# Two Strassen layers of an encoder block: a bank for the last product, weight operands made in steps, and weight sums by accumulating transfers

## The chip, the core and the metric

The kernel runs on one core of one Trainium2 chip. The metric is the device time of one execution in microseconds (us). The median of three runs of the kernel before is 1422.38 us (1410.39 to 1423.44).

## The reference, cut to what matters

One DeepNorm encoder block on 1024 tokens of width 1024: an input projection, a gated DeltaNet group beside neighbourhood attention, an output projection, and a squared-ReLU MLP. The change lies in the MLP and in what stands right ahead of it.

```python
mix = jnp.einsum('bte,ed->btd', jnp.concatenate([o_gdn, o_na], axis=-1), w_out[l])
x = layer_norm(DEEPNORM_ALPHA * x + mix, ln1_g[l], ln1_b[l])
ff = jnp.square(jax.nn.relu(jnp.einsum('btd,df->btf', x, w1[l]) + b1[l]))   # 1024 -> 4096
ff = jnp.einsum('btf,fd->btd', ff, w2[l]) + b2[l]                           # 4096 -> 1024
x = layer_norm(DEEPNORM_ALPHA * x + ff, ln2_g[l], ln2_b[l])
```

## The kernel before, in words

Every fp32 operand of a large product is split into a rounded part (fp32r, copied by ScalarE, ACT) and the rest (a subtraction on VectorE, DVE, in `sub_split`, L71). A product is then three matmuls per 128 rows: high by high, high by low, low by high.

**Both MLP layers use Winograd's form of Strassen's scheme:** a 2x2 block product with seven products in place of eight, and sums of the blocks ahead of and behind them.

**First layer.** The 4096 columns are worked in 16 pairs of 128-column blocks (`up_pair(g)`, L1013). The blocks of x (11, 21, 22 and the sums T1 to T4, each 512 channels by 512 tokens) are made once, in the stretch in which the output projection and the LayerNorm end (L944 to L974). For each pair `w1_raw` loads 1 MiB of w1, `w_ops` forms the four sums S1 to S4 (L898 to L901, DVE) and splits seven weight operands (L882 ACT, L71 DVE). The seven products have 12 matmuls each (L910 to L912): psA (11), psB6, psC7, psE5, again psA (12 times 21), psD4, and the last one, S4 times 22, which adds into psE5's bank. That bank is read by h22 = u3 + pe (L1035) ahead of it, so the last product waits for that read. Sums, bias and squared ReLU follow on DVE and ACT, and seven blocks of 256 KB go to `h_d` in DRAM (L1059). The first two products of pairs 0 and 1 are made early, between the transposes of x.

**Weight sums of the second layer.** `w2_sums(g)`, called in every pair, loads blocks of w2 (L1002, 2 x 256 KB per half pair), forms four sums on GpSimd (POOL, L1003 to L1006) and stores them in `t_d` in DRAM (L1007, 512 KB), two halves per pair, each with one buffer.

**Second layer.** Seven products in four groups of four pairs are 28 steps. Step n loads 1 MiB of `h_d` and 1 MiB of w2 or of `t_d` (`down_ops`, L1080), splits both (L1083 ACT, L71 DVE), and makes 48 matmuls (L1181 to L1183). Loads are issued two steps ahead; raw buffers turn over every three steps and the five operand tiles (`x`) hold two and a half steps.

All DMAs of the kernel before are issued by the SP queue, in order. A scheduler that simulates the program sets each engine's order; each engine then runs its own order strictly.

Of the kernel before, what the change touches and what calls it, by code (L numbers as in the profile page):

```python
# [15 lines left out]
P = 128  # L16
# [20 lines left out]
def tile_trunk(ctx: ExitStack, tc: tile.TileContext, A: dict, out: bass.AP):  # L37
# [817 lines left out]
    t_d = dr.tile([4, NG, P, 512], F32, name="t_d")  # L855
# [9 lines left out]
    for nm in ("T4", "22"):  # L865
        X[nm] = bigp.tile([P, 2, 4, 512], F32R, tag="big", name="x" + nm, bufs=2)
# [7 lines left out]
    def utile(name):  # L874
        return wk.tile([P, 512], F32, tag="u", name=name, bufs=4)
# [18 lines left out]
    def w_ops(raw, have=()):  # L894

        q11, q12, q21, q22 = (w_quad(raw, a, k) for a in range(2) for k in range(2))
        s1, s2, s3, s4 = (tmp(f"ws{i}").rearrange("p (k c) -> p k c", k=4) for i in range(4))
        V.tensor_tensor(s1, q21, q22, ALU.add)  # L898
        V.tensor_tensor(s2, s1, q11, ALU.subtract)
        V.tensor_tensor(s3, q11, q21, ALU.subtract)  # L900
        V.tensor_tensor(s4, q12, s2, ALU.subtract)  # L901
        w = dict(have)
        for nm, src in (("11", q11), ("S2", s2), ("S3", s3), ("S1", s1), ("12", q12), ("22", q22), ("S4", s4)):
            if nm not in w:
                w[nm] = w_split(src)
        return w
# [34 lines left out]
    raw1 = [tmp("w1q").rearrange("p (k c) -> p k c", k=4) for k in range(2)]  # L941
    for k in range(2):
        D.dma_start(raw1[k], A["w1"][k * 512:k * 512 + 512, 2 * P:3 * P].rearrange("(kt p) c -> p kt c", p=P))
    for hf in range(2):  # L944
        for q in range(4):
            t = hf * 4 + q
            out_proj(t, oTn[1][:, :, t * P:(t + 1) * P], wo1[0][2:4], wo1[1][2:4], oo, "o", G, nb=4)
            layer_norm(t, wk)
        for kt in range(NK) if hf == 0 else (0, 4, 1, 5, 2, 6, 3, 7):
            ps = psC.tile([P, 512], F32, tag="t", name="psx1", bufs=2)  # L950
            for q in range(4):
                mm = TE.transpose(ps[:, q * P:(q + 1) * P], yacc[hf * 4 + q][:, kt * P:(kt + 1) * P], ident)
            turns.append(mm)
            full = hold8("x1f") if hf == 0 else tmp("x1s")
            S.activation(full, ps, AF.Identity, bias=l1b[:, kt:kt + 1], scale=l1g[:, kt:kt + 1])
            k = kt % 4
            if hf == 0:
                full0[kt] = full
                x_split("11" if kt < 4 else "21", k, full, (S, V)[kt % 2], (V, G)[kt % 2])
                continue  # L960
            full1[kt] = full
            if kt < 4:
                continue
            b11, b12, b21, b22 = full0[k], full1[k], full0[kt], full
            x_split("22", k, b22, S, G)
            t1, t3 = tmp("t1"), tmp("t3")
            V.tensor_tensor(t1, b12, b11, ALU.subtract)
            V.tensor_tensor(t3, b22, b12, ALU.subtract)
            x_split("T1", k, t1, S, V)
            x_split("T3", k, t3, S, V)  # L970
            V.tensor_tensor(b22, b22, t1, ALU.subtract)
            x_split("T2", k, b22, S, V)
            V.tensor_tensor(b21, b21, b22, ALU.subtract)
            x_split("T4", k, b21, S, G)  # L974


    wops = {0: {}, 1: {}}
    for nm, src in (("11", w_quad(raw0, 0, 0)), ("12", w_quad(raw0, 0, 1))):
        wops[0][nm] = w_split(src)
    for nm, src in (("11", raw1[0]), ("12", raw1[1])):  # L980
        wops[1][nm] = w_split(src)
    early = {}
    pace = pacer(turns[NK:], 22, 3)
    for g in range(2):
        ps = bank("s", "psA")
# [4 lines left out]
    for g in range(2):  # L990
        prod(early[g][0], wops[g]["12"], X["21"], False, pace)
    close(oo)
    w2p = open_pool("w2p")
    wops[0] = w_ops(raw0, wops[0])

    def w2_sums(g):
        for hc in range(2):
            c = slice(hc * 256, hc * 256 + 256)
            r = w2p.tile([P, 2, 2, 256], F32, tag="r", name="w2r", bufs=1)
            t = w2p.tile([P, 4, 256], F32, tag="t", name="w2s", bufs=1)  # L1000
            for k in range(2):
                D.dma_start(r[:, k], A["w2"][(2 * g + k) * P:(2 * g + k + 1) * P, :].rearrange("p (j c) -> p j c", j=2)[:, :, c])  # L1002
            G.tensor_tensor(t[:, 0], r[:, 0, 1], r[:, 0, 0], ALU.subtract)  # L1003
            G.tensor_tensor(t[:, 1], r[:, 1, 1], t[:, 0], ALU.subtract)  # L1004
            G.tensor_tensor(t[:, 2], r[:, 1, 1], r[:, 0, 1], ALU.subtract)  # L1005
            G.tensor_tensor(t[:, 3], r[:, 1, 0], t[:, 1], ALU.subtract)  # L1006
            D.dma_start(t_d[:, g, :, c].rearrange("i p c -> p i c"), t)  # L1007
# [5 lines left out]
    def up_pair(g, mid=None):  # L1013
        if g + 1 < NG:
            wops[g + 1] = w_ops(w1_raw(g + 1), wops.get(g + 1, ()))
        w = wops.pop(g)
        f = 2 * g
        if g in early:
            pa, u2 = early[g]
        else:  # L1020
            pa = bank("s", "psA")
            prod(pa, w["11"], X["11"])
            u2 = utile("p1")
            S.activation(u2, pa, AF.Copy)
        pb = bank("p", "psB6")
        prod(pb, w["S2"], X["T2"])
        V.tensor_tensor(u2, u2, pb, ALU.add)
        pc = bank("t", "psC7")
        prod(pc, w["S3"], X["T3"])
        u3 = utile("u3")  # L1030
        V.tensor_tensor(u3, u2, pc, ALU.add)
        pe = bank("p", "psE5")
        prod(pe, w["S1"], X["T1"])
        h22 = hold8("h22")
        V.tensor_tensor(h22, u3, pe, ALU.add)  # L1035
        act2(h22, h22, f + 1)
        if mid is not None:
            mid()
        if g not in early:
            prod(pa, w["12"], X["21"], False)  # L1040
        h11 = hold8("h11")
        act2(h11, pa, f)
        pd = bank("o", "psD4")
        prod(pd, w["22"], X["T4"])
        h21 = hold8("h21")
        V.tensor_tensor(h21, u3, pd, ALU.add)
        act2(h21, h21, f + 1)
# [6 lines left out]
        V.tensor_tensor(s1, h12, h22, ALU.add)  # L1054
        V.tensor_tensor(s2, s1, h11, ALU.subtract)
        V.tensor_tensor(s3, h11, h12, ALU.subtract)
        V.tensor_tensor(s4, h21, s2, ALU.subtract)
        for i, h in enumerate((h11, h21, h22, s1, s2, s3, s4)):
            D.dma_start(h_d[i, g], h)  # L1059
# [4 lines left out]
    right = [t_d[i].rearrange("g p c -> p g c") for i in range(4)]  # L1064
    order = [(left[0], w2q[0, 0]), (left[4], right[1]), (left[5], right[2]), (left[3], right[0]),
             (left[2], right[3]), (left[1], w2q[1, 0]), (left[6], w2q[1, 1])]
# [3 lines left out]
    def down_ops(n):  # L1070
        i, gr = divmod(n, NQ)
        sl = slice(gr * 4, gr * 4 + 4)
        if n % 3 == 0:
            raws = [raw8().rearrange("p a (k c) -> p (a k) c", c=512) for j in range(2)]
        else:
            r = bigp.tile([P, 2, 4, 512], F32, tag="big", name="d2r", bufs=2)
            raws = [r[:, j] for j in range(2)]
        res = []
        for src, raw in zip(order[i], raws):
# [14 lines left out]
    close(w2p)  # L1094
# [202 lines left out]
```

## Time and profile before

| | |
|---|---|
| median of 3 runs | 1422.38 us |
| profiled execution | 1419.53 us, of which the span is 1417.7 us |
| mean granted TensorE clock | 0.964 |
| busy in the span: PE (TensorE) / DVE / ACT / POOL | 1303.8 / 920.5 / 639.1 / 336.5 us |
| first layer's products, first to last | 714.17 to 1098.46 us |
| second layer's products | from 1098.46 us |

Matmuls overlap, so the busy time of PE says only whether it had work; the granted clock beside it says at which of the two levels, 1.2 or 2.4 GHz, it ran. The sum of a stretch is best read from the starts of its first and last matmul.

### The profile page before, as it was taken

Reading aid. Unit: us, or ns where it says so; the run is one execution under the profiler, and the core shown is the slowest. Engines: PE = TensorE matmul, PEld = TensorE weight load, DVE = VectorE, ACT = ScalarE, POOL = GpSimd, SP = SyncE. Lnnn points to the kernel's source line nnn. Section 1 sums busy time; section 2 is a strip of 40 time slices with the busy share of each in tenths; the row PEclk is TensorE's granted clock in tenths of the full one; section 3 lists DMA queues with packets and bytes.
Section 4 is the critical chain, followed back from the end, with each engine's and each line's share of the span. In section 5 each row is a group of like instructions: output and inputs, shape, how many; then the busy total and the mean of one; then the engine's idle time right before and its main releaser. Section 6 shows DMA issues by size and latency. Waiting matters only on the chain.

```text
span 1417.7 us, 20015 instructions
## 1 busy us (share of the span) xinstructions
PE 1303.8 (92%) x7318; PEld 1082.8 (76%) x7318; DVE 920.5 (65%) x1543; ACT 639.1 (45%) x1224; POOL 336.5 (24%) x356
## 2 busy tenths in 40 slices
PE   5999999999999967999966898998799999999996
PEld 4688888878888856898745676776688788888885
DVE  6756897922368457557778766656565695555955
ACT  5457666334332253455464344353455443334431
POOL 3000001011123139223476344443300000000403
PEclk9999999989999997999987899999999999999998
DMA  6233547468776698653344677777746975555731
GB/s 188 57 110 111 141 137 170 119 135 253 229 218 201 174 343 194 172 170 100 104 144 130 231 259 231 255 232 258 233 163 223 393 270 191 207 199 178 246 111 60
DMA packets 240579, 267.27 MB, mean 189 GB/s; under 512 B 38865, under 2 KB 169809, under 8 KB 240481
## 3 DMA queue, kind: packets, MB, share of 16 engines
q1 hardware_dynamic: 240480, 265.99, 60.5%
q8 instruction: 58, 0.95, 0.3%
q14 instruction: 41, 0.33, 0.1%
HBM read 180.94 MB, written 85.00 MB: 188 GB/s over the span
## 4 chain that ended last, share of the span: by engine, by line
PE 39%; DMA 13%; DVE 7%; POOL 6%; issue 3%; ACT 2%; SPq 1%; DVEq 0%; POOLq 0%; ACTq 0%
DMA w2r<-in_w_dram 7%; PE psdn L1182 6%; PE psdn L1183 6%; PE psdn L1181 6%; DMA wraw<-in_w_dram 3%; PE po L754 2%; PE psop L802 2%; PE psop L804 2%; PE psop L803 2%; POOL w2s L1004 1%; POOL w2s L1006 1%; POOL w2s L1005 1%; POOL w2s L1003 1%; PE pt L747 1%; DMA B<-in_rpbT_dram 1%
## 5 line engine op out<-in xcount | busy, mean ns | idle before, releaser
L1182 PE MATMUL psdn<-d,d 128*128 128x512 f32 (+1 forms) x464 | 177.3, 383 | 0.8 <-DVE d L71 0.7
L1183 PE MATMUL psdn<-d,d 128*128 128x512 f32 (+1 forms) x464 | 177.1, 382 | 0.0
L1181 PE MATMUL psdn<-d,d 128*128 128x512 f32 (+1 forms) x464 | 175.1, 382 | 0.4 <-ACT d L1083 0.4
L71 DVE TENSOR_TENSOR d<-d2r,d 128x1024 fp32r<-128x1024 f32 x72 | 85.7, 1238 | 62.9 <-ACT d L1083 62.9
L1083 ACT ACTIVATE d<-d2r 128x1024 fp32r<-128x1024 f32 x72 | 71.4, 1049 | 113.0 <-PE psdn L1183 91.9
L1182 PEld LDWEIGHTS psdn<-d,d 128*128 128x128 f32 x464 | 87.3, 188 | 18.5 <-DVE d L71 1.6
L1181 PEld LDWEIGHTS psdn<-d,d 128*128 128x128 f32 x464 | 87.2, 188 | 17.7 <-ACT d L1083 0.8
L1183 PEld LDWEIGHTS psdn<-d,d 128*128 128x128 f32 x464 | 87.3, 188 | 16.6
L93 POOL TENSOR_TENSOR lrs<-lrs,mhalf 128x1 f32<-128x1 f32 x8 | 6.4, 804 | 347.8 <-DVE lrs L1123 347.8
L1010 ACT ACTIVATE h<-h,b1T 128x512 f32<-128x512 f32 x48 | 34.5, 719 | 104.2 <-DVE h L1035 76.2
L120 PE MATMUL psj<-xlo,whi 128*128 128x512 f32 x192 | 77.0, 401 | 1.8 <-DVE xlo L71 1.8
L119 PE MATMUL psj<-xhi,whi 128*128 128x512 f32 x192 | 76.4, 399 | 0.7 <-DVE xhi L170 0.7
L121 PE MATMUL psj<-xhi,wlo 128*128 128x512 f32 x192 | 75.9, 395 | 0.0
L1003 POOL TENSOR_TENSOR w2s<-w2r 128x256 f32<-128x256 f32 x32 | 29.2, 911 | 154.3 <-DMA w2r<-in_w_dram 154.3
L71 DVE TENSOR_TENSOR d<-wraw,d 128x1024 fp32r<-128x1024 f32 x40 | 47.6, 1234 | 27.8 <-ACT d L1083 27.8
L71 DVE TENSOR_TENSOR wlo<-wraw,whi 128x1024 fp32r<-128x1024 f32 x28 | 34.3, 1223 | 47.4 <-ACT whi L110 42.5
L240 DVE SCALAR_TENSOR_TENSOR cy<-hraw,convw,cy 128x1024 f32<-128x1024 f32 x48 | 61.2, 1280 | 5.6 <-ACT cy L238 4.5
L1083 ACT ACTIVATE d<-wraw 128x1024 fp32r<-128x1024 f32 x40 | 39.9, 1048 | 49.0 <-PE psdn L1183 41.5
L882 ACT ACTIVATE w1t<-ws 128x512 fp32r<-128x512 f32 x64 | 39.7, 625 | 48.3 <-PE psC L912 23.0
L898 DVE TENSOR_TENSOR ws<-wraw 128x512 f32<-128x512 f32 x16 | 11.0, 689 | 75.2 <-DMA wraw<-in_w_dram 75.2
L754 PEld LDWEIGHTS po<-vt,et 128*128 128x128 f32 x384 | 52.3, 198 | 8.7 <-ACT et L752 3.5
L754 PE MATMUL po<-vt,et 128*128 128x64 f32 x384 | 51.8, 275 | 5.1 <-ACT et L752 2.6
(341 smaller groups left out, 3679.3 us busy)
## 6 DMA issues: line engine op xcount, KB each, us to landing
wraw<-in_w_dram SPq DMA_DIRECT2D x21, 1024.0 KB, 7.0
d2r<-h_d SPq DMA_DIRECT2D x18, 1024.0 KB, 5.4
w2r<-in_w_dram SPq DMA_DIRECT2D x64, 256.0 KB, 4.3
t_d<-w2s SPq DMA_DIRECT2D x32, 512.0 KB, 3.9
h_d<-hs SPq DMA_DIRECT2D x64, 256.0 KB, 2.5
wraw<-in_w_in_dram SPq DMA_DIRECT2D x28, 512.0 KB, 4.7
h_d<-h SPq DMA_DIRECT2D x48, 256.0 KB, 5.4
d2r<-t_d SPq DMA_DIRECT2D x11, 1024.0 KB, 7.7
```

Source lines behind the costliest of these rows:

```text
L71: return eng.tensor_tensor(lo, full, f32(hi), ALU.subtract)
L119: pace(TE.matmul(ps, hi[:, kt], xhi[:, kt, sl], start=(kt == 0), stop=False))
L120: pace(TE.matmul(ps, hi[:, kt], xlo[:, kt, sl], start=False, stop=False))
L121: pace(TE.matmul(ps, lo[:, kt], xhi[:, kt, sl], start=False, stop=(kt == NK - 1)))
L240: V.scalar_tensor_tensor(y, raw[:, i:i + T], convw[:, ci, i:i + 1], y, ALU.mult, ALU.add)
L754: mm = TE.matmul(po[:, j], et[:, c], vts[j][:, t + c, e * 64:e * 64 + 64], start=(c == 0), stop=(c == 2))
L882: S.activation(t[:, 0], src, AF.Copy)
L1003: G.tensor_tensor(t[:, 0], r[:, 0, 1], r[:, 0, 0], ALU.subtract)
L1083: S.activation(t[:, 0, k], raw[:, k], AF.Copy)
L1181: TE.matmul(ps, h[:, 0, k, qs_], w[:, 0, k, c], start=(start and k == 0), stop=False)
L1182: TE.matmul(ps, h[:, 0, k, qs_], w[:, 1, k, c], start=False, stop=False)
L1183: TE.matmul(ps, h[:, 1, k, qs_], w[:, 0, k, c], start=False, stop=(stop and k == 3))
```

## The change

- **Last product:** P3 (S4 times 22) has a bank of its own (`psF3`). u2 takes psE5 by one more addition on DVE, and h12 is u2 + psF3. psA's bank alternates between two tags; the four other products share two tags.
- **First products early for four pairs** in place of two (`NE = 4`, 256 KB loads `w1q` of the pairs 1 to 3).
- **Weight operands one by one:** `w_steps` yields after each operand, and a step is written behind each join of the pair before; the 1 MiB of w1 is loaded one pair earlier.
- **x blocks:** the second token half is kept in `xs`; T1 and 22 are made first. In pair 0 the products go in the order 5, 3, 7, 6, 4. All low parts there, and those of the last output projection, are made on DVE and none on POOL.
- **Second layer's weights:** `w2_sums`, its loads, POOL sums, stores and `t_d` are gone. `down_ops` loads one block of w2 and adds 0, 2, 1, 1, 3, 0, 0 more (products 0 to 6, four steps each: 28 in all) by transfers that POOL issues and that add to the raw tile. Some sums of h and the final additions change sign for it.

```diff
-    t_d = dr.tile([4, NG, P, 512], F32, name="t_d")
...
-    def w_ops(raw, have=()):
+    def w_steps(raw, w):
...
+        V.tensor_tensor(s1, q21, q22, ALU.add)
+        put("11", q11)
+        yield
+        V.tensor_tensor(s2, s1, q11, ALU.subtract)
+        put("S2", s2)
+        yield
...
+    NE = 4
...
-            out_proj(t, oTn[1][:, :, t * P:(t + 1) * P], wo1[0][2:4], wo1[1][2:4], oo, "o", G, nb=4)
+            out_proj(t, oTn[1][:, :, t * P:(t + 1) * P], wo1[0][2:4], wo1[1][2:4], oo, "o", V, nb=4)
...
+            if kt < 4:
+                V.tensor_tensor(full0[k], full, full0[k], ALU.subtract)
+                x_split("T1", k, full0[k], S, V)
+            else:
+                x_split("22", k, full, S, V)
...
-    def w2_sums(g):
-        for hc in range(2):
-            c = slice(hc * 256, hc * 256 + 256)
...
-            D.dma_start(t_d[:, g, :, c].rearrange("i p c -> p i c"), t)
...
+        if g + 2 < NG:
+            raws1[g + 2] = w1_raw(g + 2)
+        steps = w_steps(raws1.pop(g + 1), wops[g + 1]) if g + 1 < NG else iter(())
...
-        prod(pe, w["S4"], X["22"], False)
-        h12 = hold8("h12")
-        V.tensor_tensor(h12, u2, pe, ALU.add)
-        act2(h12, h12, f)
-        w2_sums(g)
+        def p3():
+            pf = bank("t", "psF3")
+            prod(pf, w["S4"], X["22"])
+            return pf
...
+        def join5(pe):
+            V.tensor_tensor(h22, u3, pe, ALU.add)
+            V.tensor_tensor(u2, u2, pe, ALU.add)
+            act2(h22, h22, f + 1)
+            step()
...
-    order = [(left[0], w2q[0, 0]), (left[4], right[1]), (left[5], right[2]), (left[3], right[0]),
-             (left[2], right[3]), (left[1], w2q[1, 0]), (left[6], w2q[1, 1])]
+    d11, d12, d21, d22 = (w2q[k, j] for k in range(2) for j in range(2))
+    order = [(left[0], (d11,)), (left[4], (d22, d12, d11)), (left[5], (d22, d12)), (left[3], (d12, d11)),
+             (left[2], (d22, d12, d11, d21)), (left[1], (d21,)), (left[6], (d22,))]
...
-            D.dma_start(raw, src[:, sl])
+            D.dma_start(raw, src[0][:, sl])
+            for more in src[1:]:
+                G.dma_start(raw, more[:, sl], accum_op=ALU.add)
```

The order of DVE before, in the middle of the first layer (ws are the sums of the next pair, out of its load wraw; p, u and h are the joins of this pair with the banks psB, psC and psE, and hs sums of h):

```order
L898 TENSOR_TENSOR ws_9655<-wraw 128x512
L1054 TENSOR_TENSOR hs_9465<-h_9443,h_9395 128x512
L899 TENSOR_TENSOR ws_9656<-ws_9655,wraw 128x512
L71 TENSOR_TENSOR w1t<-ws_9483,w1t 128x512
L1055 TENSOR_TENSOR hs_9466<-hs_9465,h_9411 128x512
L1056 TENSOR_TENSOR hs_9467<-h_9411,h_9443 128x512
L900 TENSOR_TENSOR ws_9657<-wraw 128x512
L1027 TENSOR_TENSOR p_9524<-p_9524,psB_9526 128x512
...
L1031 TENSOR_TENSOR u_9553<-p_9524,psC_9540 128x512
L901 TENSOR_TENSOR ws_9658<-wraw,ws_9656 128x512
L71 TENSOR_TENSOR w1t<-ws_9482,w1t 128x512
L1035 TENSOR_TENSOR h_9568<-u_9553,psE_9555 128x512
```

The same place in the change:

```order
L903 TENSOR_TENSOR ws_9469<-wraw 128x512
L906 TENSOR_TENSOR ws_9470<-ws_9469,wraw 128x512
L1114 TENSOR_TENSOR hs_9280<-h_9166,h_9167 128x512
...
L1049 TENSOR_TENSOR p_9310<-p_9310,psB_9325 128x512
L909 TENSOR_TENSOR ws_9471<-wraw 128x512
L71 TENSOR_TENSOR w1t<-ws_9314,w1t 128x512
L1081 TENSOR_TENSOR u_9320<-p_9310,psC_9343 128x512
L918 TENSOR_TENSOR ws_9472<-wraw,ws_9470 128x512
L71 TENSOR_TENSOR w1t<-ws_9312,w1t 128x512
L1085 TENSOR_TENSOR h_9323<-u_9320,psE_9361 128x512
L1086 TENSOR_TENSOR p_9310<-p_9310,psE_9361 128x512
```

The sums of the next pair still stand ahead of the joins; what moved is the load behind wraw, which is issued a pair earlier, and the addition to p (L1086) that frees psE's bank from the last product.

The order of SP before around such a load (t_d is what POOL has summed, w2r the blocks for the next half):

```order
L1059 DMA h_d<-h_9395 128x512
L1007 DMA t_d<-w2s 128x4x256
L1002 DMA w2r<-in_w_dram 128x2x256 x2
L888 DMA wraw<-in_w_dram 128x8x256
L1059 DMA h_d<-h_9411 128x512
```

In the change only the seven stores to `h_d` and the load stand there, so nothing on SP waits for POOL in the first layer.

The order of POOL in the change in the second layer. It has no other instruction until the final LayerNorms; d2r_10253 is the weight tile of step 4, d2r_10316 of step 5, wraw_10392 of step 6, then steps 7, 8, 9, 10 and 11:

```order
L1143 DMA d2r_10253<-in_w2_dram 128x4x512
L1143 DMA d2r_10316<-in_w2_dram 128x4x512
L1143 DMA wraw_10392<-in_w2_dram 128x4x512
L1143 DMA d2r_10253<-in_w2_dram 128x4x512
L1143 DMA d2r_10316<-in_w2_dram 128x4x512
L1143 DMA wraw_10392<-in_w2_dram 128x4x512
L1143 DMA d2r_10455<-in_w2_dram 128x4x512
L1143 DMA d2r_10518<-in_w2_dram 128x4x512
L1143 DMA d2r_10455<-in_w2_dram 128x4x512
L1143 DMA wraw_10581<-in_w2_dram 128x4x512
L1143 DMA d2r_10655<-in_w2_dram 128x4x512
L1143 DMA d2r_10717<-in_w2_dram 128x4x512
```

Each waits until what is in its tile has landed, so the second addition of step 4 stands behind the first ones of the steps 5 and 6.

## Rows read from the trace of the kernel before

**Rows 1.** The page's 40 slices: busy tenths of PE

```profile
PE   5999999999999967999966898998799999999996
```

**Rows 2.** Busy time by stretch (length, engines, clock, DMA share, GB/s)

```profile
714.17:757.00 42.83, 20.11 (x80) 14.64 (x79) 34.10 (x37) 22.93 (x38) 30.43 (x27) 0.70 0.33 108
803.00:1098.46 295.46, 271.82 (x1136) 219.54 (x1136) 185.86 (x268) 134.23 (x218) 90.13 (x96) 0.95 0.70 230
714.17:1098.46 384.29, 332.96 (x1376) 266.71 (x1374) 251.14 (x349) 176.34 (x288) 142.02 (x140) 0.92 0.66 215
1096.00:1140.00 44.00, 43.52 (x191) 35.31 (x190) 29.98 (x30) 21.21 (x24) 0.00 (x0) 1.00 1.02 383
1160.00:1360.00 200.00, 200.00 (x884) 165.72 (x883) 128.78 (x145) 76.17 (x80) 15.89 (x12) 1.00 0.62 218
```

**Rows 3.** Waits of PE, 690 to 1160 us (total, times, longest)

```profile
PE psE L910 <- DVE h L1035: 22.3, 7, 7.4
PE psB L910 <- ACT w1t L882: 19.1, 1, 19.1
```

**Rows 4.** Chain of waits, 985 to 1020 us (start, us, what)

```profile
994.89 0.75 POOL w2s L1006
995.65 0.38 SPq L1007
...
997.46 9.46 DMA wraw<-in_w_dram
...
1015.97 0.61 DVE h L1035
```

**Rows 5.** Waits of DVE (first row) and SP (second) in the first layer

```profile
DVE ws L898 <- DMA wraw<-in_w_dram: 75.2, 13, 10.8
SPq L1007 <- POOL w2s L1006: 108.5, 31, 12.5
```

**Rows 6.** Timeline of DVE and, last, of POOL

```profile
704.93 0.42 DVE L937 CAST x<-x1f 128x512 fp32r<-128x512 f32 x1
744.25 0.68 DVE L71 TENSOR_TENSOR xT<-t,xT 128x512 fp32r<-128x512 f32 x1
744.86 1.75 DVE L967 TENSOR_TENSOR t<-x1s,x1f 128x512 f32<-128x512 f32 x1
758.71 6.68 POOL L71 TENSOR_TENSOR xT<-x1f,xT 128x512 fp32r<-128x512 f32 x1 [4.05 <-ACT xT L935]
```

**Rows 7.** Timeline of PE: first matmuls of products and of pairs

```profile
838.16 0.40 PE L910 MATMUL psA<-x,w1t 128*128 128x512 f32 x1
...
1016.62 0.79 PE L910 MATMUL psE<-x,w1t 128*128 128x512 f32 x1 [7.39 <-DVE h L1035]
...
1021.52 0.39 PE L910 MATMUL psA<-x,w1t 128*128 128x512 f32 x1
...
1040.74 0.40 PE L910 MATMUL psA<-x,w1t 128*128 128x512 f32 x1
...
1059.98 0.40 PE L910 MATMUL psA<-x,w1t 128*128 128x512 f32 x1
```

**Rows 8.** Timeline of SP: loads of the steps 1, 4 and 6

```profile
1095.85 0.37 SPq L1080 DMA_DIRECT2D d2r<-h_d  x1
...
1114.29 2.23 SPq L1080 DMA_DIRECT2D d2r<-t_d  x1
...
1130.80 2.43 SPq L1080 DMA_DIRECT2D wraw<-t_d  x1
```

**Rows 9.** The page's DMA issues (count, KB each, us to landing)

```profile
d2r<-h_d SPq DMA_DIRECT2D x18, 1024.0 KB, 5.4
d2r<-t_d SPq DMA_DIRECT2D x11, 1024.0 KB, 7.7
```

**Rows 10.** The page's costliest groups: the splits of the second layer

```profile
L71 DVE TENSOR_TENSOR d<-d2r,d 128x1024 fp32r<-128x1024 f32 x72 | 85.7, 1238 | 62.9 <-ACT d L1083 62.9
L1083 ACT ACTIVATE d<-d2r 128x1024 fp32r<-128x1024 f32 x72 | 71.4, 1049 | 113.0 <-PE psdn L1183 91.9
```

More of the change, by code (lines that the diff above doesn't have):

```diff
@@ L864, in tile_trunk @@
         X[nm] = xp.tile([P, 2, 4, 512], F32R, tag="x", name="x" + nm, bufs=5)
-    for nm in ("T4", "22"):
+    xs = bigp.tile([P, 2, 4, 512], F32, tag="big", name="xs", bufs=2)
+    for nm in ("22", "T4"):
         X[nm] = bigp.tile([P, 2, 4, 512], F32R, tag="big", name="x" + nm, bufs=2)
@@ L874, in utile @@
     def utile(name):
[L875 removed]
+        return wk.tile([P, 512], F32, tag="u", name=name, bufs=5)
     def bank(tag, name):
@@ L892, in w_quad, with put @@
         return raw[:, k * 4:k * 4 + 4, a * P:(a + 1) * P]
-    def w_ops(raw, have=()):
+    def w_steps(raw, w):
         q11, q12, q21, q22 = (w_quad(raw, a, k) for a in range(2) for k in range(2))
         s1, s2, s3, s4 = (tmp(f"ws{i}").rearrange("p (k c) -> p k c", k=4) for i in range(4))
[L898 to L903, printed above, removed]
+        def put(nm, src):
             if nm not in w:
                 w[nm] = w_split(src)
-        return w
+        V.tensor_tensor(s1, q21, q22, ALU.add)
[4 more added lines that the diff above has]
+        yield
+        V.tensor_tensor(s3, q11, q21, ALU.subtract)
+        put("S3", s3)
+        yield
+        put("S1", s1)
+        yield
+        put("12", q12)
+        yield
+        put("22", q22)
+        yield
+        V.tensor_tensor(s4, q12, s2, ALU.subtract)
+        put("S4", s4)
+        yield
     def prod(ps, w, x, first=True, pace=lambda mm: None):
@@ L962, in tile_trunk, with bank_a @@
             if kt < 4:
[L963 to L977, printed above, removed]
+                V.tensor_tensor(full0[k], full, full0[k], ALU.subtract)
+                x_split("T1", k, full0[k], S, V)
+            else:
+                x_split("22", k, full, S, V)
+    for k in range(4):
+        t1, b12, b21, b22 = full0[k], full1[k], full0[4 + k], full1[4 + k]
+        V.tensor_tensor(b12, b22, b12, ALU.subtract)
+        x_split("T3", k, b12, S, V)
+        V.tensor_tensor(t1, b22, t1, ALU.subtract)
+        x_split("T2", k, t1, S, V)
+        V.tensor_tensor(b21, b21, t1, ALU.subtract)
+    for k in range(4):
+        x_split("T4", k, full0[4 + k], S, V)
+    def bank_a(g):
+        return bank("sp"[g % 2], "psA")
+    wops = {g: {} for g in range(NG)}
     for nm, src in (("11", w_quad(raw0, 0, 0)), ("12", w_quad(raw0, 0, 1))):
         wops[0][nm] = w_split(src)
-    for nm, src in (("11", raw1[0]), ("12", raw1[1])):
-        wops[1][nm] = w_split(src)
+    for g in range(1, NE):
+        for nm, k in (("11", 0), ("12", 1)):
+            wops[g][nm] = w_split(rawq[g, k])
     early = {}
     pace = pacer(turns[NK:], 22, 3)
-    for g in range(2):
-        ps = bank("s", "psA")
+    for g in range(NE):
+        ps = bank_a(g)
         prod(ps, wops[g]["11"], X["11"], True, pace)
@@ L989, in tile_trunk @@
         early[g] = ps, u
-    for g in range(2):
-        prod(early[g][0], wops[g]["12"], X["21"], False, pace)
+        if g % 2:
+            for e in (g - 1, g):
+                prod(early[e][0], wops[e]["12"], X["21"], False, pace)
     close(oo)
-    w2p = open_pool("w2p")
-    wops[0] = w_ops(raw0, wops[0])
-    def w2_sums(g):
-        for hc in range(2):
-            c = slice(hc * 256, hc * 256 + 256)
[L999 to L1006, printed above, removed]
-            D.dma_start(t_d[:, g, :, c].rearrange("i p c -> p i c"), t)
+    raws1 = {0: raw0}
+    for _ in w_steps(raw0, wops[0]):
+        pass
+    raws1[1] = w1_raw(1)
     def act2(h, src, f):
@@ L1013, in up_pair, with step @@
     def up_pair(g, mid=None):
-        if g + 1 < NG:
-            wops[g + 1] = w_ops(w1_raw(g + 1), wops.get(g + 1, ()))
+        if g + 2 < NG:
+            raws1[g + 2] = w1_raw(g + 2)
+        steps = w_steps(raws1.pop(g + 1), wops[g + 1]) if g + 1 < NG else iter(())
+        def step():
+            next(steps, None)
         w = wops.pop(g)
@@ L1020, in up_pair @@
         else:
-            pa = bank("s", "psA")
+            pa = bank_a(g)
             prod(pa, w["11"], X["11"])
@@ new lines, in up_pair, with p6, p7, p5 @@
+        h11, h21, h22, h12 = (hold8(x) for x in ("h11", "h21", "h22", "h12"))
+        def p6():
+            pb = bank("o", "psB6")
+            prod(pb, w["S2"], X["T2"])
+            V.tensor_tensor(u2, u2, pb, ALU.add)
+            step()
+        def p7():
+            pc = bank("t", "psC7")
+            prod(pc, w["S3"], X["T3"])
+            return pc
+        def p5():
+            pe = bank("o", "psE5")
+            prod(pe, w["S1"], X["T1"])
+            return pe
+        def p2():
+            if g not in early:
+                prod(pa, w["12"], X["21"], False)
+            act2(h11, pa, f)
+            step()
@@ new lines, in p4, with join7 @@
+        def p4():
+            pd = bank("t", "psD4")
+            prod(pd, w["22"], X["T4"])
+            V.tensor_tensor(h21, u3, pd, ALU.add)
+            act2(h21, h21, f + 1)
+            step()
+        def p3():
+            pf = bank("t", "psF3")
+            prod(pf, w["S4"], X["22"])
+            return pf
+        def join7(pc):
+            V.tensor_tensor(u3, u2, pc, ALU.add)
+            step()
+        def join5(pe):
+            V.tensor_tensor(h22, u3, pe, ALU.add)
+            V.tensor_tensor(u2, u2, pe, ALU.add)
+            act2(h22, h22, f + 1)
+            step()
@@ new lines, in join3 @@
+        def join3(pf):
+            V.tensor_tensor(h12, u2, pf, ALU.add)
+            act2(h12, h12, f)
+            step()
+        if g == 0:
+            pe, pf = p5(), p3()
+            pc = p7()
+            p6()
+            join7(pc)
+            join5(pe)
+            p4()
+            p2()
+            join3(pf)
+        else:
+            p6()
+            join7(p7())
+            join5(p5())
+            if mid is not None:
+                mid()
+            p2()
+            p4()
+            join3(p3())
```

60 lines of the change are left out of this document (19 added, 41 removed).

## The prediction

> **What bounds the kernel now.** I read the page's slices first, then the stretches of the MLP, then who waited for whom, and last the chain of waits. The slices show PE full from the 30th on, where the second layer runs, and between 0.6 and 0.9 in the first layer [rows 1]. The stretches put numbers on it [rows 2]. In the second layer 884 matmuls fill 200 us, 0.226 us each at a granted clock of 1.00, that is 2.4 GHz; a step of 48 takes 10.86 us and nothing waits. In the first layer, 384.29 us long, PE is idle for 384.29 - 332.96 = 51.3 us, and the granted clock is 0.92 on average: after waits PE runs for a while at the lower level, 1.2 GHz. A pair without a wait takes 1059.98 - 1040.74 = 19.24 us for 84 matmuls, 0.229 us each [rows 7]. Sixteen such pairs are 307.8 us; the 32 transposes between them (1376 records less 1344) add some 4 (an estimate, half a matmul's time each). So 72 us of the stretch are waits and their low clock.
>
> The waits have two owners [rows 3]: one of 19.1 us at the start, while the x operands are made, and seven of the last product for h22 on DVE, 22.3 us in all. The chain shows what lies behind the second kind [rows 4]: POOL ends a sum, SP stores it, only then SP reaches the load of w1, which takes 9.46 us; DVE, which has the next pair's sums ahead of this pair's joins, stands still for it, and PE waits for the join. DVE lost 75.2 us to that load in 13 waits, SP 108.5 us to POOL in 31 [rows 5].
>
> **The change, part by part.** *Start of the first layer.* Before, the last product of pair 3 ends at 838.16 us [rows 7]. In the change about 153 DVE instructions stand between the first CAST of x, at 704.93 us, and pair 3's last join. Without POOL beside it DVE issues one every 0.61 us; next to a POOL subtraction the same form takes 1.75 in place of 0.68 us, and POOL's own took up to 6.68 [rows 6]. POOL's splits move to DVE, so its cost is in the count: 153 x 0.61 = 93, which ends at 798. PE needs 336 x 0.229 + 4 = 81 us from 714.17, to 795; the four early pairs give it 96 matmuls, 22 us, for the time in which it waited 19.1. The later bound with 5 us for arrivals is 803: a gain of 35.
>
> *Pairs 4 to 15.* Before they take 1098.46 - 838.16 = 260.3 us, without waits 12 x 19.24 = 230.9: a gain of 29. The load of w1 now has a pair's time ahead of its use. DVE's 21 instructions per pair (4 sums, 7 splits, 6 joins, one more than before, 4 sums of h) are 13 to 14 us at 0.61 to 0.68, hidden under 19.24; if a load came late again, they would be what is late. Removing POOL's 128 sums, their loads and stores has no further price: POOL was on PE's path only through SP.
>
> Of these 64 us I count 56: 8 for about four new waits of 2 us with their low clock, and for low parts of the output projection that DVE now makes ahead of 704.93. Bounds: 40, if the start gains only 11, and 68.
>
> *Second layer.* The 28 steps have 28 more transfers of 1 MiB on the same 16 engines, and POOL issues them in a strict order. No row shows an accumulating transfer. The nearest is a plain load: 383 GB/s at a share of 1.02 [rows 2] make 2.75 us per MiB, and 5.4 us to landing [rows 9] leave 2.65 us of latency. The lower end is 2.75, if only what is read from DRAM counts; the upper is 5.5, if the tile that is read back counts as much. I take the lower end, since the plain load of the same block is the nearest row, and keep both for the range.
>
> First, step 4. Its second addition stands behind the first one of step 6 on POOL, and that waits for step 6's load. From step 1's load at 1095.85 to step 6's at 1130.80 [rows 8] SP issues 16.75 MiB: 12 for the steps 1 to 6, 2.5 of constants, 1 of y and 1.25 of h. They take 46.1 us, and step 6 lands at 1095.85 + 46.1 + 2.65 = 1144.6, 46 us into the second layer. Two first additions in between make it 51.6; step 6's first and step 4's second addition, with latency, 59.8; half a split is 1.05 + 1.24 us [rows 10], so 62. PE wants step 4 after 4 x 10.86 = 43.4: a wait of 18 us. Second, product 4 (steps 16 to 19) needs 5 MiB per step, 13.75 us against 10.86, 11.6 us in all; loads run up to three steps ahead and have room in the products 2 and 3 (8.25 us per step), so I count half, 6. Third, two waits cost clock: after the wait of 7.39 us twelve matmuls took 1021.52 - 1016.62 = 4.9 us in place of 2.75 [rows 7], so 4 for two. Together 28 us.
>
> The additions and subtractions that change sign cost nothing: the same instructions in the same places.
>
> **Sum.** The profiled execution took 1419.53 us (span 1417.7), 2.85 under the median. 1419.5 - 56 + 28 = 1391 us.
>
> In the trace, plain transfers fill the engines at 383 GB/s [rows 2], and that alone gave my price. The Trainium skill (Collectives: The Full Stack, The bandwidth ceiling: the fold count and why AG ≠ RS ≠ AR) says of a transfer that adds on its way: "it's slower because the add needs **two source reads**", about half the rate of a copy. No run here shows it; by that rule the price would be the upper end, and the sum the first rival's.
>
> **Rivals.** *1. The additions bind the second layer; slower.* At 5.5 us each, the engines must carry up to step 19 16.75 + 26 plain MiB at 2.75 and 28 additions at 5.5: 117.6 + 154 = 271.6 us from 1095.85, so step 19 is ready 274 us into the layer, against 19 x 10.86 = 206 on PE. That is 68 us late, and some four waits' clock make it 76: 1419.5 - 56 + 76 = 1440. For it: the tile has to be read as well as w2, and the engines were already full for 44 us at the start of this layer. Against: their share is 0.62 later on [rows 2]. Between the ends the loss grows by (76 - 28) / 2.75 = 17.5 us per us of price; it eats the 56 at about 4.35 us, which is the point from which it decides. The page's rule above is this rival's, and its only support.
>
> *2. Gain and loss cancel.* A price near 4.1 costs 28 + 1.35 x 17.5 = 52: 1415 us. Or the first layer gains only 40, because DVE's order waits for x operands at the start: 1407. For it: DVE is the later bound there.
>
> *3. The transfers are hidden anyway.* If the additions fit under the loads, 1419.5 - 56 = 1363. For it: 0.62 of the engines' time is used in the steady part. Against: POOL's order ties step 4 to step 6 whatever the price.
>
> That the change leaves the first layer as it was is unlikely: in its order the last product has its own bank, and no load on SP stands behind POOL.
>
> **How the numbers follow.** The forecast (1375 to 1405) has a chance of 0.40, rival 3 0.10, rival 2 0.22, rival 1 0.28. A measurement of this kernel can tell about 1%, 14 us, from no change. Faster by over 1% (under 1408) are the forecast and rival 3, 0.50; within 1% 0.22; slower 0.28. The range goes from rival 3 with a first-layer gain of 64, 1356, to rival 1 with some 10 us less gain, 1450; it leaves out dearer additions still and a first layer that gains nearly nothing. Both signs hold much of the chance; the forecast's own range is 1375 to 1405.
>
> **What would show it.** In the new profile: waits of the last product for DVE gone, and the first layer's products over some 328 us long; DVE no longer waiting 75 us for w1; a wait of PE of about 18 us at step 4 and short ones at steps 16 to 19, ended by splits that waited for a POOL transfer. Waits of 10 us or more at each of the steps 16 to 19, with the DMA share near 1 there, would show rival 1. The prediction is wrong if the additions' landing time is far from 5.4 us, or if DVE holds PE in the first pairs.

## The result, and the profile after

The change takes 1429.17 us (median of 20 runs, 1424.31 to 1437.71) against 1422.36 us of the kernel before (20 runs): a ratio of 1.0084, 95% interval 1.0061 to 1.0108. The forecast was 1391, faster; the result is slower, clear of noise but by under 1%, and lies between the first rival's 1440 and the second rival's 1415. The profiled execution took 1434.19 us, span 1432.4. The two profiled executions differ by 14.7 us and the medians by 6.8: single executions of one kernel spread over more than 10 us, so the stretches below are those of one profile each.

Two stretches explain it. The first layer runs from the first matmul of its products (psA) to the first of the second layer (psdn), the second layer from there to the end of the span:

| kernel | first psA at | first layer | second layer | span |
|---|---|---|---|---|
| before | 714.2 | 384.3 | 319.2 | 1417.7 |
| the change | 712.8 | 325.6 | 394.0 | 1432.4 |
| difference | -1.4 | -58.7 | +74.8 | +14.7 |

The runs 1, 2 and 6 below have the change's first layer unaltered, and it took 326.3, 325.8 and 325.0 us there: this stretch repeats within some 1 us. The first layer gained what was forecast, the second lost 75 in place of 28. The page's slices of the change (tenths; PE, granted clock, DMA) show where: the waits stood before in the slices 21 to 29 [rows 1]; now that part is full, and holes stand where PE had been full.

```profile
PE   5999999999999966999998999999993899866996
PEclk9999999999999988999998999999996989978998
DMA  6233557469776796663314545444699999999731
```

The stretches of the change (length, busy time of PE, PEld, DVE, ACT, POOL, then clock, DMA share, GB/s), which answer to [rows 2]:

```profile
712.00:803.00 91.00, 81.38 (x349) 63.91 (x350) 79.28 (x133) 56.43 (x95) 4.16 (x6) 0.94 0.35 111
803.00:1038.00 235.00, 235.00 (x1027) 192.46 (x1026) 158.79 (x249) 124.20 (x197) 0.00 (x0) 1.00 0.51 167
1038.00:1330.00 292.00, 228.83 (x954) 185.82 (x953) 140.68 (x142) 83.62 (x88) 36.40 (x28) 0.89 1.04 275
1330.00:1420.00 90.00, 90.00 (x443) 76.37 (x441) 64.47 (x82) 34.37 (x38) 24.59 (x18) 1.00 0.41 149
```

From 803 us on PE has no idle time left in the first layer, at 2.4 GHz. In the second layer the DMA engines are full for 292 us (share 1.04) while they move 275 GB/s; full engines moved 383 before [rows 2]. So the bytes that are counted are not what fills them. When the last addition is done, PE runs full to the end. The matmuls of PE that had waited, in the timeline:

```profile
1106.19 2.07 PE L1243 MATMUL psdn<-d,d 128*128 128x512 f32 x4 [24.08 <-ACT d L1146]
...
1148.23 2.08 PE L1243 MATMUL psdn<-d,d 128*128 128x512 f32 x4 [7.49 <-ACT d L1146]
...
1258.69 2.08 PE L1243 MATMUL psdn<-d,d 128*128 128x512 f32 x4 [9.52 <-ACT d L1146]
...
1279.32 0.80 PE L1243 MATMUL psdn<-d,d 128*128 128x512 f32 x1 [7.31 <-ACT d L1146]
...
1305.80 2.08 PE L1243 MATMUL psdn<-d,d 128*128 128x512 f32 x4 [12.81 <-ACT d L1146]
...
1320.88 1.21 PE L1243 MATMUL psdn<-d,d 128*128 128x512 f32 x4 [1.45 <-ACT d L1146]
```

Counted in steps of 10.86 us from 1038.4, the first stands ahead of step 4 (1038.4 + 43.4 + 24.1 = 1105.9), the second of step 7, the last four of the steps 16 to 19. With 0.5 for a low part they are 63.2 us; the other 11.6 of the 74.8 are matmuls at the lower clock after them. The queues of the change between 1038 and 1330 us (packets, MB, share of the 16 engines' time; q0 is POOL's, q1 SP's), and two of the issues (us to landing):

```profile
q0 software_dynamic: 14784, 29.36, 55.1%
q1 hardware_dynamic: 24794, 50.81, 48.3%
...
d2r<-in_w_dram POOLq DMA_DIRECT2D x20, 1024.0 KB, 13.4
...
d2r<-in_w_dram SPq DMA_DIRECT2D x15, 1024.0 KB, 11.9
```

The 28 additions took 0.551 x 292 = 160.9 us of all engines, 5.75 us each; the 48.5 MiB of plain transfers 141 us, 2.91 each. The price is the upper end of the prediction's bounds, and a little more. The figures are shares of engines that are full; no run shows an addition on idle engines.

### The profile page after: what moved, and what is told of

Read it like the earlier page. It is cut to its first block, busy times and chain, and to the rows that moved or that the text cites. A ratio compares the mean times of both kernels' runs of the same rounds, so it can differ in the third digit from the quotient of the medians.

```text
span 1432.4 us, 19819 instructions
## 1 busy us (share of the span) xinstructions
PE 1299.7 (91%) x7318; PEld 1079.5 (75%) x7318; DVE 913.2 (64%) x1579; ACT 641.2 (45%) x1224; POOL 226.5 (16%) x236
## 3 DMA queue, kind: packets, MB, share of 16 engines
HBM read 194.58 MB, written 68.22 MB: 183 GB/s over the span
## 4 chain that ended last, share of the span: by engine, by line
PE 45%; DMA 15%; DVE 6%; issue 3%; ACT 1%; POOL 1%; SPq 0%; DVEq 0%; ACTq 0%; POOLq 0%
DMA d2r<-in_w_dram 10%; PE psdn L1243 3%; PE psdn L1244 3%; PE psdn L1245 3%; PE psA L926 2%; PE psA L924 2%; PE psA L925 2%; DMA wraw<-in_w_dram 2%; PE po L754 2%; PE psop L802 2%; PE psop L804 2%; PE psop L803 1%; PE psF L924 1%; PE psD L924 1%; PE psD L926 1%
## 5 line engine op out<-in xcount | busy, mean ns | idle before, releaser
L1243 PE MATMUL psdn<-d,d 128*128 128x512 f32 (+1 forms) x464 | 180.5, 399 | 62.7 <-ACT d L1146 62.7
L1244 PE MATMUL psdn<-d,d 128*128 128x512 f32 (+1 forms) x464 | 180.3, 389 | 0.5 <-DVE d L71 0.5
L1245 PE MATMUL psdn<-d,d 128*128 128x512 f32 (+1 forms) x464 | 179.6, 387 | 0.0
L71 DVE TENSOR_TENSOR d<-d2r,d 128x1024 fp32r<-128x1024 f32 x72 | 89.9, 1295 | 107.8 <-ACT d L1146 107.8
L1243 PEld LDWEIGHTS psdn<-d,d 128*128 128x128 f32 x464 | 90.6, 197 | 82.9 <-ACT d L1146 65.2
L1143 POOL DMA_DIRECT2D d2r<-in_w_dram x20 | 26.6, 1359 | 519.0 <-DMA bB<-in_ln_b_dram 347.8
L1244 PEld LDWEIGHTS psdn<-d,d 128*128 128x128 f32 x464 | 89.4, 193 | 19.2 <-DVE d L71 1.5
L1245 PEld LDWEIGHTS psdn<-d,d 128*128 128x128 f32 x464 | 89.1, 192 | 17.6
L743 ACT ACTIVATE ex<-sn,nm 128x384 f32<-128x384 f32 x64 | 39.0, 609 | 33.9 <-DVE nm L739 18.4
L802 PE MATMUL psop<-wo,oh 128*128 128x512 f32 x128 | 53.1, 418 | 0.2 <-ACT oh L796 0.2
L803 PE MATMUL psop<-wo,oh 128*128 128x512 f32 x128 | 51.6, 403 | 0.0
## 6 DMA issues: line engine op xcount, KB each, us to landing
d2r<-in_w_dram POOLq DMA_DIRECT2D x20, 1024.0 KB, 13.4
```

The lines of the kernel that those rows point to most:

```text
L71: return eng.tensor_tensor(lo, full, f32(hi), ALU.subtract)
L802: pace(TE.matmul(ps, oh[:, k], hi[k][:, c], start=(k == 0), stop=False))
L803: pace(TE.matmul(ps, oh[:, k], lo[k][:, c], start=False, stop=False))
L1243: TE.matmul(ps, h[:, 0, k, qs_], w[:, 0, k, c], start=(start and k == 0), stop=False)
L1244: TE.matmul(ps, h[:, 0, k, qs_], w[:, 1, k, c], start=False, stop=False)
L1245: TE.matmul(ps, h[:, 1, k, qs_], w[:, 0, k, c], start=False, stop=(stop and k == 3))
```

## Experiments

Ratios are against runs of the kernel before on the same chip. The profiles' first layers start anywhere from 700.9 to 716.5 us, so the stretches are compared and not the spans alone.

**1. No additions.**

```diff
-            for more in src[1:]:
-                G.dma_start(raw, more[:, sl], accum_op=ALU.add)
```

> The change without its 28 accumulating transfers; the base block alone is loaded, so the sums of w2 blocks are left out. Theory A (the additions cost the whole loss): the second layer goes back to PE's pace, some 75 us shorter than in the change, and the first layer keeps its gain of 60: about 1357 us, no wait of PE for a split in the second layer. Theory B (part of the loss is elsewhere, in the order of the loads or in the low clock after the first layer): 1375 to 1400 us, with waits of PE that stay.

Measured: 1356.09 us, ratio 0.9569 [0.9517, 0.9620]; first layer 326.3, second 319.4. Its stretch from 1031 us:

```profile
1031.00:1330.00 299.00, 297.91 (x1334) 246.66 (x1333) 195.43 (x213) 116.63 (x124) 16.71 (x14) 1.00 0.58 212
```

Theory A holds: the whole loss of the second layer goes with the additions. The order of SP's loads costs nothing.

**2. The same transfers as plain copies.**

```diff
-                G.dma_start(raw, more[:, sl], accum_op=ALU.add)
+                G.dma_start(raw, more[:, sl])
```

> The same 28 transfers from POOL, of the same blocks into the same tiles with the same waits, as plain copies: each overwrites the tile, so the sums are left out. Theory A (the addition itself doubles the time on the DMA engines, 5.7 us for 1 MiB in place of 2.9): the DMA engines' share falls to about 0.75 in the second layer and the time to 1385 to 1393 us, as the prediction had it at 2.75 us per transfer. Theory B (it is POOL's queue, its issue and its strict order, not the addition): 1420 to 1432 us, as the change.

Measured: 1382.47 us, ratio 0.9753 [0.9701, 0.9806]; first layer 325.8, second 345.4. Its queues between 1039 and 1300 us:

```profile
q1 hardware_dynamic: 27423, 55.96, 58.9%
q0 software_dynamic: 7616, 29.36, 29.9%
```

The 28 copies took 0.299 x 261 = 78.0 us, 2.79 each: the same blocks, tiles, queue and order of issue at half the price. Packets are 272 per copy and 528 per addition. They are not the price: SP's plain transfers have some 512 per MiB too (24794 in 48.5 MiB) and cost 2.91 us. The page counts 194.58 MB read from DRAM in both kernels, so if an addition reads twice, the second reading is not one of DRAM; no view shows that reading itself. PE's waits with the copies:

```profile
1099.03 2.08 PE L1243 MATMUL psdn<-d,d 128*128 128x512 f32 x4 [14.82 <-ACT d L1146]
...
1261.67 2.08 PE L1243 MATMUL psdn<-d,d 128*128 128x512 f32 x4 [7.61 <-ACT d L1146]
```

Theory A holds. This kernel is also the prediction's second layer at the prediction's price: 14.8 at step 4 (18 forecast), 7.6 in product 4 (6), some 4 of clock (4), 26 in all (28).

**3. The sums of before in the change's first layer.** The same loads, four sums (with the signs of the change) and stores, called in every pair; the second layer loads `t_d`.

```diff
+        w2_sums(g)
         s1, s2, s3, s4 = (hold8(f"hs{i}") for i in range(4))
```

> The first layer of the change with the weight sums of before: loads of w2, sums on POOL, stores to DRAM from SP in every pair, no accumulating transfers. Theory A (the first layer's gain comes from the early load and does not need POOL to be idle): first layer 330 to 340 us long, second layer as before, 1362 to 1380 us. Theory B (the gain came from taking POOL's sums and their stores off SP): the waits for w1 come back, first layer 350 to 380 us, 1385 to 1415 us.

Measured: 1423.34 us, ratio 1.0026 [0.9994, 1.0058]; first layer 394.5, second 319.1. Theory A falls: with these sums the new first layer is no shorter than the old one, and longer than theory B had it (350 to 380). Waits of SP and DVE in it, then its timeline where it starts, of POOL, SP, DVE and PE:

```profile
SPq L1034 <- POOL w2s L1033: 137.1, 31, 23.2
```

```profile
DVE ws L904 <- DMA wraw<-in_w_dram: 87.2, 13, 19.4
```

```profile
731.68 18.51 POOL L1030 TENSOR_TENSOR w2s<-w2r 128x256 f32<-128x256 f32 x1 [4.31 <-DMA w2r<-in_w_dram]
```

```profile
727.84 0.68 DVE L71 TENSOR_TENSOR x<-xs,x 128x512 fp32r<-128x512 f32 x1
728.44 0.68 DVE L71 TENSOR_TENSOR xT<-x1f,xT 128x512 fp32r<-128x512 f32 x1
...
748.91 0.68 DVE L71 TENSOR_TENSOR xT<-xs,xT 128x512 fp32r<-128x512 f32 x1
769.03 0.69 DVE L904 TENSOR_TENSOR ws<-wraw 128x512 f32<-128x512 f32 x1 [19.44 <-DMA wraw<-in_w_dram]
```

```profile
752.39 0.38 SPq L1034 DMA_DIRECT2D t_d<-w2s  x1
...
761.92 0.59 SPq L889 DMA_DIRECT2D wraw<-in_w_dram  x1
```

```profile
772.79 0.80 PE L926 MATMUL psB<-xT,w1t 128*128 128x512 f32 x1 [22.18 <-DVE xT L71]
```

The chain of [rows 4] is back, and longer: a POOL sum (L1030, 0.74 us in the median) takes 18.51 while DVE issues one SBUF instruction after another, and ends 0.6 us after the last of them; SP's store waits for it; the load of w1 stands behind the store; DVE waits 19.44 us for the load, with the x operands queued behind that; PE waits 22.18 us.

**4. No bank of its own.**

```diff
-            pf = bank("t", "psF3")
-            prod(pf, w["S4"], X["22"])
+            prod(pe, w["S4"], X["22"], False)
...
-            V.tensor_tensor(u2, u2, pe, ALU.add)
```

> The change with its last product back in psE's bank, behind the join of h22, and without the addition that frees that bank. Theory A (with the load a pair ahead DVE joins in time, and the bank is worth little): 1426 to 1434 us, first layer within 4 us of the change's 325.6. Theory B (the bank is what took the seven waits of 22 us away): they come back with their low clock, first layer 345 to 355 us, 1450 to 1460 us.

Measured: 1425.56 us, ratio 1.0058 [1.0023, 1.0092]; first layer 322.1, second 399.3. No last product waits for a join. Theory A: where the loads come in time, the bank is worth nothing in the first layer. Why the second layer, which the edit leaves alone, is 5 us longer stays open; the interval overlaps the change's.

**5. The sums on POOL's own queue.** Sums in place in a tile of four blocks, two such tiles; POOL issues loads and stores. A copy of one column of pair 1's h12 into the first tiles keeps the sums out of the start.

```diff
+            t = w2p.tile([P, 4, 256], F32, tag="t", name="w2s", bufs=2)
...
+                G.dma_start(t[:, 2 * k:2 * k + 2], A["w2"][(2 * g + k) * P:(2 * g + k + 1) * P, :].rearrange("p (j c) -> p j c", j=2)[:, :, c])
+            for to, by in ((0, 1), (1, 3), (3, 0), (2, 3)):
+                G.tensor_tensor(t[:, to], t[:, to], t[:, by], ALU.add)
+            G.dma_start(t_d[:, g, :, c].rearrange("i p c -> p i c"), t)
```

> The weight sums on POOL once more, made in place in two buffers of four blocks, from pair 1 on, with loads and stores issued by POOL, so that nothing on SP waits for POOL; no accumulating transfers. Theory A (in the run with POOL's sums the loss came from SP standing behind POOL's stores): DVE no longer waits for w1, first layer 328 to 340 us, 1358 to 1378 us. Theory B (POOL's sums themselves slow DVE, or DVE starves POOL and the sums come too late for the steps 4 to 7): first layer 345 us or more, or waits of 10 us and more at the steps 4 to 7, 1385 to 1420 us.

Measured: 1370.11 us, ratio 0.9683 [0.9643, 0.9724]; first layer 330.1, second 330.6. Theory A holds for the first layer: the same sums as in run 3, 64 us shorter. Queue, second buffer and later start changed together here; run 8 takes the queue alone. PE's waits show what is left in the second layer: a late low part, first as a sum of PE's waits, then in the timelines of DVE and PE:

```profile
PE psdn L1262 <- DVE d L71: 8.9, 3, 6.8
```

```profile
1083.97 0.69 DVE L1181 TENSOR_SCALAR gB<-gB 128x1024 f32<-128x1024 f32 x1 [6.14 <-DMA gB<-in_ln_g_dram]
1084.69 11.31 DVE L1187 TENSOR_TENSOR yr<-yr,gB 128x1024 f32<-128x1024 f32 x8
1095.93 1.21 DVE L71 TENSOR_TENSOR d<-d2r,d 128x1024 fp32r<-128x1024 f32 x1
```

```profile
1097.20 0.79 PE L1262 MATMUL psdn<-d,d 128*128 128x512 f32 x1 [6.84 <-DVE d L71]
```

DVE stood 6.14 us for a constant of the LayerNorm (gB), then made eight products with it, and the low part that PE wanted stood behind them.

**6. Plain copies, added by DVE.**

```diff
-                G.dma_start(raw, more[:, sl], accum_op=ALU.add)
+                one = fp.tile([P, 4, 512], F32, tag="one", name="w2one", bufs=2)
+                G.dma_start(one, more[:, sl])
+                for k in (slice(0, 2), slice(2, 4)):
+                    V.tensor_tensor(raw[:, k], raw[:, k], one[:, k], ALU.add)
```

> The change with its 28 additional blocks loaded as plain copies into two tiles of their own (POOL's queue) and added to the raw tile by DVE, 56 additions of 128x1024. Theory A (the price is the addition on the DMA engines; DVE has room at 128.8 us busy of 200): some 70 us more DVE work that hides, 1372 to 1392 us, as the plain copies. Theory B (DVE becomes late: loads, additions and splits in one chain): PE waits at most steps of the products 1, 2 and 4, 1400 to 1430 us.

Measured: 1391.10 us, ratio 0.9850 [0.9822, 0.9879]; second layer 353.2, 8 more than the bare copies. Theory A, at its upper edge. DVE is now busy for 222.28 of 274 us, and 9.2 us of PE's waits are for low parts on DVE:

```profile
1026.00:1300.00 274.00, 246.53 (x1055) 200.37 (x1054) 222.28 (x226) 94.28 (x100) 30.39 (x35) 0.95 0.85 312
```

**7. The kernel before without its sums.**

```diff
-        w2_sums(g)
```

> The kernel before with the weight sums left out: no w2 loads, POOL sums or stores in the first layer; the second layer loads plain blocks of w2 where the sums stood. Theory A (the prediction's split: 35 of the gain are the start, from the order of the x operands and four early pairs, 29 the pairs): the start's wait of 19 us stays, the pairs run free, first layer about 350 us, 1385 to 1392 us. Theory B (nearly all of the gain is the sums' removal from POOL and SP): first layer 325 to 335 us, 1355 to 1370 us.

Measured: 1362.45 us, ratio 0.9631 [0.9584, 0.9678]; first layer 331.4, second 319.1. Theory B: of the 58.7 us that the first layer gained, 52.9 come by taking the sums away from the kernel before, and 5.8 more by all else (bank, steps, early pairs, x order). This order of counting matters: with the sums left in, all else gained nothing (run 3). Counted from the first matmul of pair 4 on, the twelve later pairs take 230.9 us here and in the change, against 260.3 before; the start takes 100.5 us here, 94.7 in the change and 124.0 before. So all of the 5.8 lies in the start. The waits of PE and of DVE in this run:

```profile
PE psB L910 <- ACT w1t L882: 14.9, 1, 14.9
```

```profile
DVE ws L898 <- DMA wraw<-in_w_dram: 32.4, 12, 4.8
```

**8. The kernel before, its sums issued by POOL.**

```diff
-                D.dma_start(r[:, k], A["w2"][(2 * g + k) * P:(2 * g + k + 1) * P, :].rearrange("p (j c) -> p j c", j=2)[:, :, c])
+                G.dma_start(r[:, k], A["w2"][(2 * g + k) * P:(2 * g + k + 1) * P, :].rearrange("p (j c) -> p j c", j=2)[:, :, c])
...
-            D.dma_start(t_d[:, g, :, c].rearrange("i p c -> p i c"), t)
+            G.dma_start(t_d[:, g, :, c].rearrange("i p c -> p i c"), t)
```

> The kernel before with one edit: the loads and stores of the weight sums are issued by POOL and not by SP; sums, buffers and start as before. Theory A (the coupling of SP to POOL is the loss): the pairs 4 to 15 run at 19.2 to 20 us, DVE's waits for w1 fall from 75 to 30 to 40 us; the start may keep its wait or lose some us more, since the x splits on POOL now stand behind these waits: first layer 335 to 350 us, 1370 to 1388 us. Theory B (POOL's sums as such slow the pairs): first layer 365 us or more, 1400 to 1420 us.

Measured: 1394.46 us, ratio 0.9816 [0.9739, 0.9894]; first layer 355.4, second 327.2. Neither theory alone: of the 53 us of the sums 29 go when SP has neither their loads nor their stores, and 24 stay, 10 of them in the start and 14 in the later pairs. The waits of DVE are between those of [rows 5] and the run without sums. A DVE instruction with two inputs in SBUF is slower than there, one that reads a bank (L1031) is not. L900 is one of the two lines that lose most; over all lines with two SBUF inputs between 840 and 1030 us the mean is 772 ns here and 687 there. How the 24 us divide between POOL's work beside DVE, the sums' transfers and their single buffers is not shown; POOL's work alone does not make them, since in run 5 POOL makes 26 of the 32 half pairs' sums beside DVE in the first layer, which is 4.5 us longer than without them. Here (busy, mean ns):

```profile
DVE ws L898 <- DMA wraw<-in_w_dram: 56.0, 13, 6.9
```

```profile
L900 DVE TENSOR_TENSOR ws<-wraw 128x512 f32<-128x512 f32 x10 | 9.5, 952 | 0.0
...
L1031 DVE TENSOR_TENSOR u<-p,psC 128x512 f32<-128x512 f32 x10 | 6.8, 677 | 0.0
```

And in the run without sums:

```profile
L1031 DVE TENSOR_TENSOR u<-p,psC 128x512 f32<-128x512 f32 x10 | 6.8, 681 | 1.4 <-PE psC L912 1.4
...
L900 DVE TENSOR_TENSOR ws<-wraw 128x512 f32<-128x512 f32 x8 | 5.5, 683 | 0.0
```

The Trainium skill (SBUF — State Buffer, Who interferes with whom) says that a DVE instruction with two SBUF inputs contends with a GpSimd instruction that reads SBUF. These rows agree: 952 against 683 ns with two, 677 against 681 with one.

**9 to 12. Four more forms of the sums on POOL's queue.** Run 9 puts those of run 5 into the kernel before, from pair 0's h22 on; run 10 is run 5 with that start; run 11 is run 10 with one bank; run 12 has one bank, run 5's start, and the product with d21 second. The first lines are run 10 against run 5, the last one is of run 12.

```diff
-        if g > 0:
-            w2_sums(g - 1, h12 if g == 1 else None)
-        if g == NG - 1:
-            w2_sums(g)
+        w2_sums(g, h22 if g == 0 else None)
...
+    turn = (0, 5, 1, 2, 3, 4, 6)
```

> The kernel before with the weight sums made in place in two buffers, issued by POOL, from the h22 of pair 0 on; everything else of its first layer as before. Theory A (the new first layer of the change is worth some 6 us, as the run without sums has it): first layer 333 to 342 us, second layer 319 to 330, 1365 to 1380 us, at most 10 us behind the same sums in the change's first layer. Theory B (the bank and the operands one by one matter once POOL disturbs DVE): 1385 us or more.

> As the run with the sums on POOL's own queue, but from the h22 of pair 0 on, some 12 us earlier, so that the last sums land before step 7 wants them. Theory A: second layer 319 to 324 us in place of 330.6, first layer 328 to 334: 1355 to 1368 us. Theory B (DVE's dense stretch at the start keeps POOL from starting, and nothing is won): 1365 to 1375 us.

> The same with the last product back in psE's bank and without the addition that frees it: 16 DVE instructions of 0.61 us less. Theory A (the bank is worth nothing when loads come in time): within 5 us of the run with the bank. Theory B (POOL's sums delay DVE's joins, and the last product waits again for the join of h22): waits of the last product on DVE of 10 us and more, 1370 to 1385 us.

> The change's first layer with one bank, the sums on POOL's own queue from the h12 of pair 1 on, and the second layer's products in another order: the one with d21 (which needs no sum) second, so that the first sums are wanted at step 8 and not at step 4. Theory A (what the second layer lost to late sums, 9 to 12 us, goes; the first layer stays at 325 to 331 us): second layer 319 to 322 us, 1352 to 1366 us. Theory B (the second layer's loss is the stores' traffic beside the loads and not the order): second layer 327 to 331 us, 1367 to 1376 us.

| run | us | ratio, 95% interval | first layer | second layer |
|---|---|---|---|---|
| 9 | 1381.07 | 0.9741 [0.9678, 0.9804] | 351.0 | 323.0 |
| 10 | 1377.31 | 0.9699 [0.9645, 0.9754] | 344.0 | 324.5 |
| 11 | 1372.79 | 0.9662 [0.9597, 0.9727] | 329.6 | 328.2 |
| 12 | 1380.26 | 0.9753 [0.9696, 0.9811] | 339.6 | 324.4 |

Three of the four came out later than their theory A, and met no theory B either (run 9: 1385 or more; run 10: 1365 to 1375; run 12: a second layer of 327 to 331); run 11 is within the 5 us of run 10 that its theory A had. The second layers of 10 and 12 did get shorter than run 5's, but their first layers did not hold 330 us: the last product waited for DVE again, with a bank of its own (run 10, first row) and without (run 12):

```profile
PE psF L925 <- DVE u L1095: 13.9, 6, 5.1
```

```profile
PE psE L925 <- DVE h L1098: 11.6, 6, 4.2
```

The intervals of the runs 5 and 10 to 12 overlap, so they are not told apart. The first layers differ in the twelve later pairs: 235.6 and 237.2 us in the runs 5 and 11, 249.5 and 248.5 in 10 and 12. What makes them differ stays open: neither the bank nor the start of the sums goes with it alone. Run 5 (1370.11 us) or run 11 is the version to take; both are clear of the kernel before and of the change.

## Why the prediction was wrong

**The step that failed is the price of an accumulating transfer**: "I take the lower end, since the plain load of the same block is the nearest row". It is 5.75 us for 1 MiB, not 2.75. Run 2 isolates it: without the addition the same 28 transfers cost 2.79 us each. The nearest row was near in bytes, not in the work of the engines. The row that I preferred held no addition at all. The rule of the Trainium skill beside that step (Collectives: The Full Stack, The bandwidth ceiling: the fold count and why AG ≠ RS ≠ AR: two source reads, about half the rate), stated there for a ReduceScatter, gave the other price. In time the runs agree: 5.75 / 2.79 = 2.06. That a second reading is what costs it, no run here shows.

**The first rival was right**, in cause and size: it had 76 us for the second layer, and 74.8 were lost; it put all of it on the DMA engines, and their share was 1.04. By the ratio alone, gain and loss nearly cancelled, as the second rival had it, but at a price of 5.75 and not of 4.1. The first rival's mark of 10 us or more at each of the steps 16 to 19 did not come: more than a third (24.1) fell at step 4, 7.5 at step 7, and those four had 9.5, 7.8, 12.8 and 1.5. Of the 6 us by which its 1440 was above the profiled execution, 4 are the first layer's. The Trainium skill was not its only support, as the prediction has it: the engines' share of 1.02 at the start of this layer [rows 2] pointed the same way.

**The sum with the measured price comes out somewhat high.** The prediction's slope of 17.5 us per us of price gives 28 + 3.0 x 17.5 = 80.5 us for 5.75, and 74.8 were measured; with its own gain of 56 that makes 1419.5 - 56 + 80.5 = 1444, against 1434.19 for the profiled execution. So the price carries nearly all of the miss, and the path from price to loss was about right.

**First layer: the size was right, the reason mostly not.** 56 was counted, 58.7 measured; 328 us forecast, 325.6 measured. At 803 us some 19 matmuls of the first four pairs were left (1027 records for 12 x 84 = 1008), so they ended near 807, a gain of 29 and not 35; the twelve others took 231 us, a gain of 29, as forecast, and needed nothing of the reserve of 8. So 56 came this near partly by luck: the start gained less than counted, and the reserve made up for it. The upper bound of 68 has no working. The prediction credited the start to x operands made on DVE and to early pairs. Run 7 has neither, keeps its wait of 14.9 us, and is 6 us longer, all of it in the start; its later pairs are as fast without an early load or a bank. Run 4 has no bank and is no longer.

**"POOL was on PE's path only through SP" was half right.** Run 8 takes SP off that path and gains 29 of 53 us; what makes the other 24 is not shown, but they go with the sums. And the early load did not protect by itself: in run 3 it stood behind POOL all the same.

**Step 4, product 4 and the clock** were right as mechanisms, as run 2 shows at the price assumed. The landing time that the prediction named as a sign (5.4 us) was 13.4 for the additions, but 9.1 for run 2's copies too: on full engines it does not tell the price.

**The third rival** (hidden transfers, 1363) fell: the additions had no cover. Without them the change takes 1356.

## What to carry to other kernels

Price an accumulating transfer from DRAM to SBUF as two transfers on the DMA engines until a trace of your own shows its price, and judge engines by their busy share, not by GB/s: 275 GB/s was all they gave. Before a layer is rebuilt, leave the suspected work out of the old one for one run: here that gave 53 of 59 us and named the sums as the cause; moving them to another queue then showed that SP's wait for POOL was some 29 of them. Work that can be late belongs on a queue behind which nothing urgent stands.

## What the runs showed of the hardware

- An accumulating transfer of 1 MiB from DRAM to SBUF took 5.75 us of all 16 engines and 528 packets while the engines were full (the change); a plain one from the same queue 2.79 us and 272 (run 2); one from SP's queue 2.91 us and some 512 (the change).
- A sum of 128x256 on POOL, 0.74 us in the median, took 18.51 us while DVE issued SBUF instructions at 0.60 us without a gap, and ended 0.6 us after the last (run 3). That it was kept out by the whole run of them, and not by one, is argued from this one event.
- Beside POOL's sums DVE's 128x512 instructions with two SBUF inputs took 772 in place of 687 ns on average, 952 in place of 683 at line L900; those that read a PSUM bank took 676 to 679 in place of 680 to 688 (run 8 against run 7).
